# Seven-product units in four more projections of a two-layer trunk, and a second clock for the mixers' steps

## The chip, the cores and the metric

The kernel runs on one core of a Trainium2 chip. The metric is the device time of one execution in microseconds; of several runs the median counts. One run was recorded by the hardware profiler, and the profile and the trace below are of that run.

## The reference

The reference is a decoder trunk of two layers over 256 tokens of width 2048, all in float32. Cut to what matters:

```
for l in range(2):
    h = rms_norm(x)                                  # 256 x 2048
    q, k, v, uv, gate_logits = split(h @ w_in[l])    # widths 1024, 256, 256, 2048, 4096
    a = attention(rope(norm(q)), rope(norm(k)), v) @ w_attn_branch[l]
    b = spatial_gating(gelu(uv)) @ w_sgu_branch[l]
    x = x + (sigmoid(g1) * a + sigmoid(g2) * b) @ w_out[l]
    h2 = rms_norm(x)
    x = x + (silu(h2 @ w_gate[l]) * (h2 @ w_up[l])) @ w_down[l]
```

The attention has 16 query heads on 4 key heads of 64, a window of 128 and a learned sink per head. The spatial gating normalises its second half v in groups of 128 channels, mixes it over the positions of a chunk of 128 with one 128x128 matrix per group, and multiplies it by the first half u.

## The kernel before

**Matmuls.** All 256 tokens are worked on at once, as two tiles of 128. The big products are cut into jobs: one job is 1024 columns of a weight matrix (two chunks c of 512), or 512 for keys and values. A job runs over units of 512 rows of the weight; w_in has four units, the two branch projections have two. Each float32 operand is split into a high and a low part of the type that TensorE takes at full rate, and one product is three matmuls: high by high, high by low, low by high (`three`, L345). The token blocks are the stationary operand (uh, ul), the weight parts the moving one (whi, wlo).

**Weight parts.** A weight tile of 256 rows by 512 columns (128 partitions x 1024 numbers) is one part. For each part ScalarE writes the high part (whi, L226) and VectorE the low one (wlo, L234). `Stream` orders this: before the matmuls of part n, `fill` (L238) queues the low of the part four places on, and its five buffers (N_LOW) let the next low begin when the oldest part has been used.

**Whole units and seven-product units.** A whole unit of a wide job has four parts of 12 matmuls each. A job with m=1 does its first unit by Strassen's scheme instead (L371 to L390): seven parts named 11, t1, t2, 21, t3, 22, t4 of 6 matmuls each, that is 42 matmuls for 48. For it VectorE makes four differences of weight tiles (`add`, L214) and, after t4, adds a fifth product to two accumulators (L386); ScalarE copies an accumulator three times (L380) and the fifth product once (L383). The token side needs sums of its blocks, split into sh and sl, which `combine` (L450) makes once per normalised input. In the kernel before, m=1 holds for the second pair of gates, w_out and the feed-forward block, and not for queries, v, u and the first pair of gates (M_GATE at L45).

**The order of the work.** Each engine's queue follows the order in which the program names the instructions. `tick` (L296) advances a slot number by 1 after each part of a whole unit and by 0.5 after each of the seven products; `after(n, fn)` (L263) lays a step down n slots on, `soon` (L266) ahead of the next part's matmuls. The mixers' steps are laid down so: the rotation of queries and keys (`rotate`, L722), the eight groups of scores (`begin`, L775, one every Q_STEP = 4 slots, with their steps at L847), the gelu (L857), the centring of v (L888) and the spatial mixing (L919). Their results leave PSUM through three buffers (tag "at"); the big products use five accumulators.

**Jobs of a layer, in order:** keys/values (KV), queries (Q), v (V), u (U), first gates (ga0, ga1), attention branch (A0, A1), second gates and spatial branch in turn, w_out, then the feed-forward rounds. In the second layer Q comes ahead of KV. At the start of layer 0 the input is transposed on TensorE while KV runs (L595 to L601).

## Time and profile before

| | us |
|---|---|
| three runs | 2490.21, 2488.70, 2490.82 |
| median | 2490.21 |
| the profiled run, whole | 2486.52 |
| its span, first to last instruction | 2484.8 |
| TensorE busy | 2464.7 (99%) |
| VectorE busy | 1901.5 (77%) |
| ScalarE busy | 1359.2 (55%) |
| GpSimd busy | 479.5 (19%) |

A row of the timeline gives the start, the duration and the instruction, with the idle time before it and what ended it. A row of a group (by line and shape) gives the count, the busy time, the mean of one in ns and the idle time before. A row of the windows gives a stretch, its length, and each engine's busy time in it. Matmuls overlap, so what one costs is the distance between two starts and not its own duration.

### The profile page before, as it was taken

The page shows a single profiled execution, that of the slowest core. Times are in us where ns is not written, and L with a number is a line of the kernel's source. Part 1 is how long each engine was busy: PE and PEld are TensorE (multiplying, and loading weights), DVE is VectorE, ACT ScalarE, POOL GpSimd, SP SyncE. Part 2 cuts the span into 40 slices and gives each one's busy share as a digit, 9 for nine tenths or more (in the row PEclk, how much of TensorE's full clock was granted, in tenths as well). Part 3 has the DMA queues.
Part 4 walks back from the last instruction along what each step waited for, and adds up shares of the span by engine and source line. Part 5 has one row for each costly group of instructions (what it writes and reads, how often), then busy time and mean ns, then how long its engine had stood idle before and what let it go on. Part 6 is the DMA issues. An engine that isn't in the chain of part 4 may idle for free. (4 is left out here: it accounts for less than half of the span.)

```text
span 2484.8 us, 30610 instructions
## 1 busy us (share of the span) xinstructions
PE 2464.7 (99%) x11030; PEld 2023.1 (81%) x11030; DVE 1901.5 (77%) x2135; ACT 1359.2 (55%) x1660; POOL 479.5 (19%) x911
## 2 busy tenths in 40 slices
PE   9999999999999999999999999999999999999999
PEld 7888887788888888888888888877888888888887
DVE  6796667787877787777878956678878776877686
ACT  5455455576655555455654544555756555645554
POOL 1512202231220022002235122022402200220020
PEclk9999999999999999999999999999999999999999
DMA  8645656666565656566676546565756656565654
GB/s 280 227 157 169 204 196 205 205 200 223 195 233 173 234 187 233 191 219 206 216 231 214 166 160 214 192 201 187 251 189 230 211 197 209 196 221 184 213 192 164
DMA packets 161880, 507.71 MB, mean 204 GB/s; under 512 B 22016, under 2 KB 24672, under 8 KB 161728
## 3 DMA queue, kind: packets, MB, share of 16 engines
q1 hardware_dynamic: 133408, 476.87, 56.7%
q0 software_dynamic: 28000, 28.62, 3.8%
q8 instruction: 86, 1.41, 0.2%
q14 instruction: 66, 0.54, 0.1%
q10 hardware_dynamic: 320, 0.27, 0.0%
HBM read 475.27 MB, written 2.10 MB: 192 GB/s over the span
## 5 line engine op out<-in xcount | busy, mean ns | idle before, releaser
L234 DVE TENSOR_TENSOR wlo<-raw,whi 128x1024 fp32r<-128x1024 f32 (+1 forms) x940 | 1129.5, 1217 | 502.7 <-PE acc L347 415.8
L226 ACT ACTIVATE whi<-raw 128x1024 fp32r<-128x1024 f32 (+1 forms) x940 | 983.3, 1056 | 843.0 <-PE acc L348 773.6
L346 PE MATMUL acc<-whi,uh 128*128 128x512 f32 x3164 | 1243.2, 393 | 7.1 <-DVE acc L386 4.6
L347 PE MATMUL acc<-wlo,uh 128*128 128x512 f32 x3164 | 1232.7, 390 | 3.1 <-DVE wlo L234 3.1
L348 PE MATMUL acc<-whi,ul 128*128 128x512 f32 x3164 | 1232.3, 389 | 0.0
L438 POOL DMA_DIRECT2D tt<-blk x800 | 393.1, 498 | 1721.8 <-DVE blk L432 1042.6
L346 PEld LDWEIGHTS acc<-whi,uh 128*128 128x128 f32 x3164 | 594.2, 188 | 146.2 <-DVE acc L386 13.1
L348 PEld LDWEIGHTS acc<-whi,ul 128*128 128x128 f32 x3164 | 594.4, 188 | 125.0
L347 PEld LDWEIGHTS acc<-wlo,uh 128*128 128x128 f32 x3164 | 594.6, 188 | 124.0 <-DVE wlo L234 3.7
L226 ACT ACTIVATE whi<-sum 128x1024 fp32r<-128x1024 f32 x84 | 89.2, 1062 | 96.6 <-PE acc L348 61.2
L346 PE MATMUL acc<-whi,sh 128*128 128x512 f32 x336 | 132.7, 395 | 5.0 <-ACT acc L380 5.0
L347 PE MATMUL acc<-wlo,sh 128*128 128x512 f32 x336 | 131.0, 390 | 0.0
L348 PE MATMUL acc<-whi,sl 128*128 128x512 f32 x336 | 130.9, 390 | 0.0
L234 DVE TENSOR_TENSOR wlo<-sum,whi 128x1024 fp32r<-128x1024 f32 x84 | 102.5, 1221 | 8.7 <-PE acc L347 8.7
L346 PEld LDWEIGHTS acc<-whi,sh 128*128 128x128 f32 x336 | 63.0, 188 | 23.7 <-ACT acc L380 11.1
L380 ACT ACTIVATE acc<-acc 128x512 f32<-128x512 f32 x126 | 73.7, 585 | 10.0 <-PE acc L348 10.0
L348 PEld LDWEIGHTS acc<-whi,sl 128*128 128x128 f32 x336 | 63.1, 188 | 13.4
L347 PEld LDWEIGHTS acc<-wlo,sh 128*128 128x128 f32 x336 | 63.1, 188 | 12.5
L538 DVE TENSOR_TENSOR ul<-tt,uh 128x1024 fp32r<-128x1024 f32 x38 | 46.4, 1222 | 17.9 <-ACT uh L535 16.1
L535 ACT ACTIVATE uh<-tt 128x1024 fp32r<-128x1024 f32 x38 | 40.3, 1059 | 34.6 <-DMA tt<-blk 32.5
L386 DVE TENSOR_TENSOR acc<-acc,p 128x512 f32<-128x512 f32 x84 | 54.1, 689 | 0.0
L218 DVE TENSOR_TENSOR raw<-raw,sum 128x1024 f32<-128x1024 f32 x42 | 51.4, 1224 | 1.4
(134 smaller groups left out, 1055.0 us busy)
## 6 DMA issues: line engine op xcount, KB each, us to landing
raw<-in_w_in_dram SPq DMA_DIRECT2D x112, 1024.0 KB, 5.1
raw<-in_w_down_dram SPq DMA_DIRECT2D x88, 1024.0 KB, 6.7
raw<-in_w_gate_dram SPq DMA_DIRECT2D x80, 1024.0 KB, 6.0
raw<-in_w_up_dram SPq DMA_DIRECT2D x80, 1024.0 KB, 6.2
raw<-in_w_out_dram SPq DMA_DIRECT2D x32, 1024.0 KB, 6.8
tt<-blk POOLq DMA_DIRECT2D x800, 32.0 KB, 5.1
raw<-in_w_attn_branch_dram SPq DMA_DIRECT2D x16, 1024.0 KB, 6.2
raw<-in_w_sgu_branch_dram SPq DMA_DIRECT2D x16, 1024.0 KB, 5.8
```

What stands on the lines that cost most here:

```text
L218: nc.vector.tensor_tensor(out=self.raw(dst), in0=self.raw(total[0]), in1=self.raw(total[1]), op=ALU.subtract)
L226: nc.scalar.activation(hi[:, k, :], raw[:, k, :], AF.Copy)
L234: nc.vector.tensor_tensor(out=lo[:, k, :], in0=raw[:, k, :], in1=hi[:, k, :].bitcast(F32), op=ALU.subtract)
L346: nc.tensor.matmul(ps, a, hi, start=first, stop=False, skip_group_check=True)
L347: nc.tensor.matmul(ps, a, lo, start=False, stop=False, skip_group_check=True)
L348: nc.tensor.matmul(ps, b, hi, start=False, stop=last, skip_group_check=True)
L380: nc.scalar.activation({"11": x, "t2": e, "t3": y}[name], a, AF.Copy)
L386: nc.vector.tensor_tensor(out=d, in0=d, in1=fifth, op=ALU.add)
L438: nc.gpsimd.dma_start(blocks(d)[:, :, i] if whole else d[:, i].rearrange("p k t c -> p (k t) c"), src)
L535: nc.scalar.activation(blocks(unit.hi), tv, AF.Copy)
L538: nc.vector.tensor_tensor(out=blocks(unit.lo), in0=tv, in1=blocks(unit.hi).bitcast(F32), op=ALU.subtract)
```

## The change

1. Queries, v, u and the first job of the first gates get m=1 in both layers. The sums of the first token unit are therefore made early: in layer 0 at slot 4, while KV runs; in layer 1 with the unit itself, at the end of layer 0. The separate `add_sums` after the first gates goes.
2. A second clock, `calm`, counts the parts of whole units only and stands still in the seven products. The steps of rotation, scores, gelu, centring and mixing are laid down on it instead of on slots. Groups of scores follow each other every 3 steps (4 before); the transposed weights come at +8 (+6), the values at +10 (+9), the gathering of the result at +9 (+7).
3. The evictions of queries, keys, v and u go through `evicting`, which before a seven-product job spreads the second chunk over 1.5 slots.
4. The raw spatial matrices get a buffer of the big pool in place of two small ones, the small tiles of the scores get four buffers, and the eight warm-up matmuls of 128 columns become two of 512.

```diff
-Q_STEP = 4
+Q_STEP = 3
-M_GATE, M_ATT, M_SGU = (0, 0, 1, 1), (0, 0), (0, 0)
+M_Q, M_V, M_U = 1, 1, 1
+M_GATE, M_ATT, M_SGU = (1, 0, 1, 1), (0, 0), (0, 0)
...
+    def calm(n, fn):
+
+        calm_steps.append((calm_no[0] + n, fn))
...
     def tick(n=1, first=None):
         slot_no[0] += n
+        calm_no[0] += n == 1
         if first is not None:
             first()
-        due = [s for s in steps if s[0] <= slot_no[0]]
-        steps[:] = [s for s in steps if s[0] > slot_no[0]]
-        for _, fn in sorted(due, key=lambda s: s[0]):
-            fn()
+        for clock, waiting in ((slot_no, steps), (calm_no, calm_steps)):
+            due = [s for s in waiting if s[0] <= clock[0]]
+            waiting[:] = [s for s in waiting if s[0] > clock[0]]
+            for _, fn in sorted(due, key=lambda s: s[0]):
+                fn()
...
-                    after(1 + i + late, step)
-            after(9 + late, then)
+                    calm(1 + i + late, step)
+            calm(9 + late, then)
...
-                        after(n, lambda t=t, g=g: self.scores(t, g))
+                        calm(n, lambda t=t, g=g: self.scores(t, g))
                         n += Q_STEP
-                after(n + 7, lambda c=c: transposed(self.attT, c, self.att[c], sums=c == 0 and sum(M_ATT)))
+                calm(n + 9, lambda c=c: transposed(self.attT, c, self.att[c], sums=c == 0 and sum(M_ATT)))
...
-            for n, step in ((1, masked), (2, exps), (4, inverse), (6, weights), (9, values), (10, weighted)):
-                after(n, step)
+            for n, step in ((1, masked), (2, exps), (4, inverse), (8, weights), (10, values), (11, weighted)):
+                calm(n, step)
...
-            soon(halved)
+            evicting(c, halved, ahead=squared)
             for i, fn in enumerate((inner, tanh, outer)):
-                after(1 + i, fn)
+                calm(1 + i, fn)
...
-                after(4 + 3 * t + 6 * c, lambda t=t: self.center(c, t))
+                calm(4 + 3 * t + 6 * c, lambda t=t: self.center(c, t))
...
-            after(2, normed)
+            calm(2, normed)
...
+        if not l:
+            after(4, lambda nrm=norm: nrm.add_sums(0))
         for done in (kv_done, q_done)[::-1 if l else 1]:
             run(norm.units, done)
...
-        after(2, lambda nrm=norm: nrm.add_sums(0))
...
-                residual(hT, nxt, False, out if nxt is None else None)
+                residual(hT, nxt, M_Q, out if nxt is None else None)
```

More of the change, by code (lines that the diff above doesn't have):

```diff
@@ L321, in hybrid_trunk @@
     nc.scalar.activation(table, warm[:, :1], AF.Copy)
-    pw_ = ps_at.tile([P, P], F32, tag="at", name="pwarm")
-    for i in range(N_WARM):
-        nc.tensor.matmul(pw_, warm, warm, start=True, stop=True)
+    pw_ = ps_acc.tile([P, CW], F32, tag="acc4", name="pwarm")
+    for i in range(N_WARM // 4):
+        nc.tensor.matmul(pw_.rearrange("p (a b) -> p a b", b=P), warm, warm.unsqueeze(1).to_broadcast([P, 4, P]),
+                         start=True, stop=True)
     pf = ps_at.tile([P, CW], F32, tag="at", name="pf")
@@ L659, in fetch @@
             if i < 2:
-                self.wr[i] = wr_ = temp((P, 4, P), "wsraw")
+                if i == 0:
+                    self.both = slot([P, 2, 4, P], name="wsraw")
+                self.wr[i] = wr_ = self.both[:, i]
                 eng.dma_start(wr_, w_spatial[l, 4 * i:4 * i + 4].rearrange("g i j -> i g j"))
@@ L789, in scores @@
             pr4 = pr.rearrange("p i j k -> p (i j) k")
-            nm_, es, den, rd = (tiny(4, w) for w in ("negm", "es", "den", "rd"))
+            nm_, es, den, rd = (tiny(4, w, 4) for w in ("negm", "es", "den", "rd"))
             pss = []
@@ L855, in __init__, with gelu, halved, squared @@
             self.vt, self.sguT = [None] * 2, [None] * 2
-        def gelu(self, ps, dst):
+        def gelu(self, c, ps, dst):
             sq = slot([P, NT, CW], name="sq")
-            for t in range(NT):
+            def halved(t):
+                nc.vector.tensor_scalar(out=dst[:, t, :], in0=ps[t], scalar1=self.nrm.rh[t], scalar2=None, op0=ALU.mult)
+            def squared(t):
                 nc.scalar.activation(sq[:, t, :], ps[t], AF.Square, scale=self.nrm.r[t])
-            def halved():
-                for t in range(NT):
-                    nc.vector.tensor_scalar(out=dst[:, t, :], in0=ps[t], scalar1=self.nrm.rh[t], scalar2=None,
-                                            op0=ALU.mult)
             def inner():
@@ L908, in normed @@
                 nc.vector.tensor_tensor(out=vt[:, t, :], in0=vt[:, t, :], in1=self.pl.lnb[:, sl], op=ALU.add)
-            after(2, normed)
+            calm(2, normed)
         def u(self, c, ps):
             ut = slot([P, NT, CW], name="u")
-            self.gelu(ps, ut)
+            self.gelu(c, ps, ut)
             for b in range(2):
-                after(12 + 3 * b + 6 * c, lambda b=b: self.mix(c, b, ut))
-            after(19 + 6 * c, lambda: transposed(self.sguT, c, ut, sums=c == 0 and sum(M_SGU)))
+                calm(12 + 3 * b + 6 * c, lambda b=b: self.mix(c, b, ut))
+            calm(19 + 6 * c, lambda: transposed(self.sguT, c, ut, sums=c == 0 and sum(M_SGU)))
         def mix(self, c, b, ut):
@@ L933, in gated @@
                                                    op0=ALU.add, op1=ALU.mult)
-            after(1, gated)
+            calm(1, gated)
     def residual(units, nxt, sums, out_at=None, scale=None):
```

19 lines of the change are left out of this document (10 added, 9 removed).

## The prediction, made before the changed kernel ran

> **What bounds the kernel now.** I read the page first, then windows over single jobs, then the timeline of VectorE where a seven-product job begins, then the groups by shape.
>
> ```profile
> span 2484.8 us, 30610 instructions
> PE 2464.7 (99%) x11030; PEld 2023.1 (81%) x11030; DVE 1901.5 (77%) x2135; ACT 1359.2 (55%) x1660; POOL 479.5 (19%) x911
> ```
>
> TensorE is hardly ever idle. Whether the change pays hangs on two things: how many matmuls go, and whether VectorE, at 77% on average, can still feed TensorE where they go. The windows show both (length, then each engine's busy time): layer 1's queries, U, the first gates, and an existing seven-product job (gb0).
>
> ```profile
> 1248.75:1292.27 43.52, 43.52 (x193) 36.04 (x192) 28.26 (x35) 24.28 (x31) 16.72 (x35) 1.00 0.71 232
> 1359.33:1412.68 53.35, 53.35 (x274) 43.31 (x272) 50.25 (x112) 31.07 (x64) 6.62 (x4) 1.00 0.46 157
> 1412.68:1469.78 57.10, 57.10 (x298) 47.06 (x298) 41.43 (x63) 32.57 (x66) 7.91 (x16) 1.00 0.51 163
> 1561.51:1603.67 42.16, 42.16 (x187) 34.91 (x186) 26.08 (x24) 23.64 (x26) 0.00 (x0) 1.00 0.67 226
> ```
>
> A plain job of 192 matmuls takes 43.52 us, 0.2267 each; a seven-product job of 186 takes 42.16. U is 9.8 us longer than a plain job because the mixers' own matmuls stand in it, and in U VectorE is busy 50.25 of 53.35 us already. Yet lows are not late today:
>
> ```profile
> L347 PE MATMUL acc<-wlo,uh 128*128 128x512 f32 x3164 | 1232.7, 390 | 3.1 <-DVE wlo L234 3.1
> ```
>
> Those 3.1 us fall at the start of the kernel. So the gain is plain and the question is the seam, the passage into seven products. VectorE's timeline at gb0, which starts at 1561.51:
>
> ```profile
> 1561.56 1.23 DVE L234 TENSOR_TENSOR wlo<-raw,whi 128x1024 fp32r<-128x1024 f32 x1 [0.75 <-PE acc L347]
> 1562.70 1.22 DVE L218 TENSOR_TENSOR sum<-raw,raw 128x1024 f32<-128x1024 f32 x1
> 1563.84 0.68 DVE L1018 SCALAR_TENSOR_TENSOR gate<-gate,acc 128x512 f32<-128x512 f32 x1
> 1564.43 1.22 DVE L234 TENSOR_TENSOR wlo<-raw,whi 128x1024 fp32r<-128x1024 f32 x1
> 1565.57 1.22 DVE L234 TENSOR_TENSOR wlo<-sum,whi 128x1024 fp32r<-128x1024 f32 x1
> 1566.70 0.68 DVE L1018 SCALAR_TENSOR_TENSOR gate<-gate,acc 128x512 f32<-128x512 f32 x1
> 1567.30 4.62 DVE L234 TENSOR_TENSOR wlo<-raw,whi 128x1024 fp32r<-128x1024 f32 x4
> 1571.85 1.28 DVE L386 TENSOR_TENSOR acc<-acc,p 128x512 f32<-128x512 f32 x2
> ```
>
> This is the best case. VectorE had been waiting 0.75 us for a free buffer, so it is as far ahead as five buffers allow: at the job's start the lows of 11, t1, t2 and 21 lie ready and that of t3 begins. Each wide instruction holds the queue 1.14 us (1562.70 to 1563.84), a half-wide one 0.6. The seven products last 42 x 0.2267 = 9.52 us, one whole part 2.72. The fifth-product additions end at 1573.05, and TensorE needs them after t4 and one whole part, at 1561.51 + 9.52 + 2.72 = 1573.75. **The seam has 0.7 us to spare even when VectorE begins it with a full head start.** Whatever VectorE is behind at the start of seven products, less 0.7, becomes TensorE idle time. Calling the low of t3 "due" when it is needed, here it is 1561.56 + 1.2 against 1561.51 + 4 x 1.36 = 1566.95: 4.2 us ahead.
>
> **The change, part by part.**
>
> *What goes.* Eight jobs (Q, V, U, ga0 in two layers) lose 6 matmuls each: 8 x 1.36 = **10.9 us**. The Trainium skill (TensorE: Matmul & The Clock Gate, Back-to-back issue gap) gives some 131 ns as the sustained spacing of matmuls of 512 columns in a stream with weight loads; by that the 48 matmuls would be an estimated 6.3 us. The trace's 227 ns per matmul disagrees, and it decides.
>
> *What comes to VectorE.* Per job three lows more, four differences (1.14 each) and two additions (0.6 each): 9.1 us, in jobs that are 1.36 us shorter. The calm clock moves no mixer work into the seven products, but it squeezes the same work into the 12 whole parts that remain, and what stands in the last four whole parts ahead of the next seam is queued ahead of the low of t3 there. From the low of 11 to that of t3 VectorE makes four lows and two differences, 6.8 us, while the uses lie 4 x 1.36 = 5.44 apart. So
>
> lead(t3) = lead(11) + 5.44 - 6.8 - (mixer work of those four parts),
>
> with lead(11) = 9.6 at a full head start (four whole parts less one low), and the job then stalls 4.2 - lead(t3) - 0.7. The mixer work by rows of the groups:
>
> ```profile
> L893 DVE BATCH_NORM_STATS2 bst<-v 128x6 f32<-128x128 f32 x32 | 8.5, 266 | 0.0
> L894 DVE BATCH_NORM_AGGREGATE mv<-bst 128x2 f32<-128x6 f32 x32 | 5.8, 182 | 1.1
> L903 DVE TENSOR_SCALAR v<-v,mv,rv 128x128 f32<-128x128 f32 x32 | 8.8, 337 | 0.0
> L907 DVE TENSOR_TENSOR v<-v,ln 128x512 f32<-128x512 f32 x8 | 5.5, 693 | 0.3
> L803 DVE TENSOR_TENSOR pr<-psc,mask 128x512 f32<-128x512 f32 x16 | 10.3, 683 | 0.0
> L806 DVE TENSOR_REDUCE mx<-pr 128x4 f32<-128x1024 f32 x8 | 9.8, 1220 | 0.3
> L819 DVE RECIPROCAL rd<-den 128x4 f32<-128x4 f32 x16 | 2.8, 178 | 0.6
> L864 DVE TENSOR_SCALAR u<-acc,rhalf 128x512 f32<-128x512 f32 x8 | 5.6, 743 | 0.0
> L868 DVE SCALAR_TENSOR_TENSOR sq<-sq,u 128x1024 f32<-128x1024 f32 x4 | 4.9, 1216 | 0.0
> L739 DVE TENSOR_TENSOR q<-q,rq 128x1024 f32<-128x1024 f32 x4 | 4.8, 1212 | 0.0
> L745 DVE TENSOR_TENSOR sq<-q,sa 128x512 f32<-128x512 f32 x8 | 5.1, 681 | 0.0
> L750 DVE TENSOR_TENSOR q<-q,ca 128x1024 f32<-128x1024 f32 x4 | 4.9, 1216 | 0.0
> L756 DVE TENSOR_TENSOR q<-q,sq 128x1024 f32<-128x1024 f32 x4 | 5.8, 1442 | 0.0
> L432 DVE STREAM_TRANSPOSE blk<-q 128x512 f32<-128x512 f32 x8 | 5.2, 682 | 0.0
> ```
>
> Counting calm steps from KV = 8 (layer 0) gives Q 8 to 20, V to 32, U to 44, ga0 to 56, ga1 to 72; layer 1 has the same numbers from V on.
>
> - *U to ga0, both layers.* Calm 42 to 44 hold: centring of v's second chunk 4 x (266 + 182), a wide mask 2 x 683 + 1220 and small ones like the 178 ns reciprocal (0.5 together), the two evictions of u's first chunk 2 x 743, gelu's inner step 1216, normalising 4 x 337 + 2 x 693: 10.6 us, 9.5 when 0.08 is taken off for each that starts before its neighbour ends. Lead(11): in U the seam leaves the first whole part about 2 us ahead; twelve parts (32.6) and about 4.6 us of the mixers' matmuls (of U's 9.8) follow, against 12 lows, one difference and the fifth-product additions (16.0) and 15.1 us of calm 33 to 39 (four gelu steps, two centrings, two normalisings, two narrow masks of about half the wide one; overlap taken off): about 8. Lead(t3) = 8 + 5.44 - 6.8 - 9.5 = -2.9, against +4.2. Stall 6.4, of which the values matmuls that stand after the first whole part cover 0.5: **5.9**.
> - *The wait behind it.* The scores of calm 44 hold two of the three small PSUM buffers until their mask at calm 45, the values of calm 45 take the third. The weights of calm 46 must wait for that mask, which VectorE reaches after one low, centring, reciprocal, two gelu steps and half the mask: about 6 us after the additions, when TensorE is one part and the values further on (3.2). Price **2.8**, between 0 (the work already drained) and 6. Everything behind it on TensorE's queue waits too. Before, with 4 slots from scores to scores, this did not occur.
> - *V to U, layer 0.* Calm 29 to 32: rotation's 2 x 681, 1216, 1442, gathering 2 x 682, eviction of v 2 x 743 (as u), inner 1216: 8.1, less overlap 7.4. Lead(11) is 9.6 less 1.0: the two parts before carry a rotation step each and the second also a difference, 1.14 + 1.2 against 2.72 - 1.14 = 1.58 to spare. Lead(t3) = 8.6 + 5.44 - 6.8 - 7.4 = -0.2; stall **3.7**. In layer 1 the queries' rotation is long done there: no stall.
> - *KV to V, layer 1.* Calm 17 to 20 hold the second query chunk's reduction (as the 1220 one), 1216, 1442, gathering and 1212: 6.6, less overlap 6.2. Lead(11) is 9.6 less 0.7 for the same reason, with one such part. Lead(t3) = 8.9 + 5.44 - 6.8 - 6.2 = 1.3; stall **2.2**.
> - *Q to V in layer 0 and the residual to Q in layer 1:* little work ahead, **0.1** and **0.4**.
>
> *The start.* In layer 0 the sums of the first token unit are due for t1 of Q, with three differences queued by then. VectorE today, from a low that ends at 29.07 to the four-ahead low that ends at 38.97, and TensorE where t1's third matmul (the first with sl) would stand:
>
> ```profile
> 29.07:38.97 9.90, 9.90 (x48) 8.27 (x47) 8.60 (x31) 8.26 (x14) 1.76 (x2) 1.00 0.79 293
> ```
>
> ```profile
> 39.52 0.39 PE L348 MATMUL acc<-whi,ul 128*128 128x512 f32 x1
> ```
>
> ```profile
> L462 DVE TENSOR_TENSOR sums<-full 128x256 f32<-128x256 f32 x4 | 1.7, 418 | 0.0
> ```
>
> VectorE has 1.3 us of idle time in that stretch. Added are: full 1.14, four sums 4 x 0.34, sl 1.14, three differences 3.4, together 7.05; with 0.4 of the idle time filled sl is ready at 45.6. TensorE waits **6.1** (part of it earlier, since the last token unit's lows stand in the same queue). Then lows of t3 to w4 (seven, 8.0), a difference, the keys' evictions and small ones (2.9) and the additions 1.2 end at 57.7; TensorE, from 45.6, would want them at 45.6 + 0.9 + 6.8 + 2.72 = 56.0: **1.7** more. Start: 7.8.
>
> *Costed at nothing.* ScalarE's three highs and four copies per job (about 5 us; it is busy 31 to 33 of U's and ga0's 53 to 57, but where it waits for VectorE's differences, the seam's sum has that). The later gathering of the attention result (calm 68): GpSimd, busy 6.62 and 7.91 us in U's and ga0's windows, has its queue free, and by the slots the unit is there as A0's second half begins; a slot too late would cost 2.72 once per layer. The powers and gathers of rotation, on the same GpSimd queue, keep their distances in whole parts. The warm-up: same columns. More live tiles in the big pool could add waits; no row shows the price, between 0 and one VectorE step (1.2) per group of scores, and I take 0.
>
> *Sum.* Stalls 7.8 + 0.1 + 3.7 + 2 x (5.9 + 2.8) + 0.4 + 2.2 = 31.6; less 10.9: +20.7. On the profiled run, 2486.52 whole for a span of 2484.8: 2507.2. That run is 3.7 below the median of 2490.21, so the median becomes **2510.9**.
>
> **Rivals.** 0.2% of this time, 5 us, is about what a measurement can tell from no change.
> - *Seams and start covered* (faster): if under about 3.9 us of mixer work stands in the last four whole parts of each job, lead(t3) stays at 3.5 or more, and if the sums finish by 39.5 the start costs nothing. Then only 0.4 remains of the stalls: 2490.2 - 10.5 = 2479.7. For it: VectorE's average over Q to ga1 stays under TensorE's time. Against: 9.5, 7.4 and 6.2 us at three seams, by rows.
> - *Seams covered, start not:* -10.9 + 7.8 + 0.4: 2487.5, no change.
> - *The clock drops:* today TensorE has stood still 2.55 us at the start without slowing:
>
> ```profile
> 16.91 0.50 PE L347 MATMUL acc<-wlo,uh 128*128 128x512 f32 x1 [2.55 <-DVE wlo L234]
> 17.25 0.40 PE L348 MATMUL acc<-whi,ul 128*128 128x512 f32 x1
> 17.48 0.40 PE L346 MATMUL acc<-whi,uh 128*128 128x512 f32 x1
> ```
>
> The start's 6.1 us may come in one piece or two. If a longer stop slows the next 16 or so matmuls to twice 0.23, one such stop adds some 3.6 us: 2514.5. The Trainium skill (TensorE: Matmul & The Clock Gate, What's actually happening) has that rule: after an idle window of about 3.4 us the clock halves until a busy one has passed; the row above, shorter than that, does not test it.
>
> **How the numbers follow.** Forecast 0.67, covered 0.14, start alone 0.11, clock 0.08. The first and the last are slower: 0.75; no change 0.11; faster 0.14. The range: low 2490, which is the forecast without the buffer waits (5.6) and with every seam 3 us lighter (15); high 2523, the forecast with a dropped clock and a pool wait of 1.2 for each of the eight score groups. It leaves out the two covered cases.
>
> **What would show it.** TensorE idle before t1 of layer 0's Q, ended by VectorE's sl or ScalarE; rows of idle time at L346 and L347 ended by wlo and L386 in both ga0, in U of layer 0 only, in V of layer 1 only; ga1 without idle time; weights (L827) waiting after ga0's first whole parts; plain stretches of 42.17 us elsewhere. If ga0 runs without stalls, the ledger of calm 42 to 44 is wrong; if t1 does not wait, the start is.

## The result, and the profile after

| | before | after |
|---|---|---|
| median of four runs, us | 2489.45 | 2521.07 |
| lowest to highest | 2487.23 to 2490.82 | 2519.32 to 2522.96 |
| the profiled run, whole | 2486.52 | 2522.01 |
| its span | 2484.8 | 2520.3 |

The changed kernel is slower: the ratio is 1.0128, with a 95% interval of 1.0110 to 1.0146. The forecast was 2510.9 in a range of 2490 to 2523. Between the two medians the difference is 31.6 us, between the two profiled runs 35.5, where the forecast's sum had 20.7.

The page of the changed kernel, its span and the engines:

```profile
span 2520.3 us, 30675 instructions
PE 2472.7 (98%) x10970; PEld 2017.8 (80%) x10970; DVE 1971.0 (78%) x2206; ACT 1396.4 (55%) x1716; POOL 479.6 (19%) x911
```

VectorE does 69.5 us more work, but as a share of the longer span it went from 77% to 78%. An average cannot show what happened. The windows over the same four jobs as in the prediction (queries, U and first gates of layer 1, then gb0):

```profile
1271.00:1315.90 44.90, 43.27 (x187) 34.60 (x187) 35.67 (x44) 30.73 (x43) 16.78 (x35) 1.00 0.74 247
1384.80:1433.70 48.90, 47.75 (x224) 37.17 (x222) 47.83 (x88) 28.55 (x49) 8.36 (x11) 1.00 0.53 178
1433.70:1499.20 65.50, 58.49 (x297) 46.35 (x295) 54.36 (x91) 38.65 (x81) 2.29 (x4) 0.97 0.46 154
1596.90:1639.00 42.10, 42.10 (x187) 34.89 (x186) 26.10 (x24) 23.64 (x26) 0.00 (x0) 1.00 0.68 227
```

gb0 is as it was. The queries take 1.4 us more, although six matmuls went. The first gates take 8.4 us more. U takes 4.5 less, but only because mixers' matmuls moved from it into later jobs: it has 50 matmuls fewer (224 for 274), and the seven products account for 6 of them. In the first gates the granted clock is 0.97, where it was 1.00.

TensorE's groups by shape (count, busy, mean ns, then the idle time ahead of them and what ended it), first one row of the kernel before, then the changed kernel's:

```profile
L346 PE MATMUL acc<-whi,sh 128*128 128x512 f32 x336 | 132.7, 395 | 5.0 <-ACT acc L380 5.0
```

```profile
L355 PE MATMUL acc<-whi,uh 128*128 128x512 f32 x3084 | 1215.6, 394 | 8.6 <-DVE acc L395 4.9 <-ACT whi L227 1.7 <-ACT uh L498 1.6
L356 PE MATMUL acc<-wlo,uh 128*128 128x512 f32 x3084 | 1204.3, 391 | 2.8 <-DVE wlo L235 2.8
L355 PE MATMUL acc<-whi,sh 128*128 128x512 f32 x400 | 161.4, 403 | 25.3 <-ACT acc L389 24.3 <-DVE u L871 0.9
L357 PE MATMUL acc<-whi,sl 128*128 128x512 f32 x400 | 158.0, 395 | 1.3 <-DVE sl L466 1.3
L838 PE MATMUL ppt<-ident,pr 128*128 128x128 f32 x96 | 13.1, 273 | 4.1 <-DVE pr L814 4.1
```

The matmuls against the sums (whi,sh) open the products t1, t2, t3 and 22. TensorE stood idle ahead of them for 5.0 us in the kernel before, already then for ScalarE's copies (L380), and stands idle for 25.3 now. What ends the wait is not a low part (the row of wlo,uh still has 2.8) but ScalarE's copy of an accumulator, L389. Before t2 may be added to the accumulator that holds product 11, ScalarE must have copied 11 out of it; the same goes for t3. Why those copies are late is seen in ScalarE's timeline where U of layer 0 begins, at 135.20. Product 11 ends near 136.6:

```profile
136.40 0.67 ACT L874 ACTIVATE sq<-acc,rstd 128x512 f32<-128x512 f32 x1
139.00 1.06 ACT L881 ACTIVATE sq<-sq 128x1024 f32<-128x1024 f32 x1 [1.93 <-DVE sq L877]
139.97 1.04 ACT L227 ACTIVATE whi<-raw 128x1024 fp32r<-128x1024 f32 x1
140.91 0.58 ACT L389 ACTIVATE acc<-acc 128x512 f32<-128x512 f32 x1
141.43 0.66 ACT L874 ACTIVATE sq<-acc,rstd 128x512 f32<-128x512 f32 x1
143.53 1.06 ACT L227 ACTIVATE whi<-sum 128x1024 fp32r<-128x1024 f32 x1 [1.44 <-DVE sum L219]
144.50 1.04 ACT L227 ACTIVATE whi<-raw 128x1024 fp32r<-128x1024 f32 x1
145.44 0.58 ACT L389 ACTIVATE acc<-acc 128x512 f32<-128x512 f32 x1
```

The first copy (140.91) stands behind gelu's tanh (L881), which waited 1.93 us for a step of VectorE's, and behind a high part. The second (145.44) stands behind the high part of a difference that VectorE had not made. So VectorE's lateness reaches TensorE by way of ScalarE's queue, before any low part is missed. VectorE began the low of t2 at 132.97, and t2 could start only at 141.54:

```profile
132.97 1.22 DVE L235 TENSOR_TENSOR wlo<-raw,whi 128x1024 fp32r<-128x1024 f32 x1
141.54 0.80 PE L355 MATMUL acc<-whi,sh 128*128 128x512 f32 x1 [3.49 <-ACT acc L389]
```

Behind the copies stands VectorE itself. From the start of U to 204.60, near the end of ga0's seven products, it is busy for 68.23 of 69.40 us (the third of the busy times), TensorE for 61.72:

```profile
135.20:204.60 69.40, 61.72 (x263) 47.74 (x262) 68.23 (x114) 43.09 (x72) 14.15 (x19) 0.93 0.47 156
```

### The profile page after: what moved, and what is told of

Same layout as the page of the kernel before. It is cut to its first block, busy times and chain, and to the rows that moved or that the text cites. A ratio compares the mean times of both kernels' runs of the same rounds, so it can differ in the third digit from the quotient of the medians.

```text
span 2520.3 us, 30675 instructions
## 1 busy us (share of the span) xinstructions
PE 2472.7 (98%) x10970; PEld 2017.8 (80%) x10970; DVE 1971.0 (78%) x2206; ACT 1396.4 (55%) x1716; POOL 479.6 (19%) x911
## 5 line engine op out<-in xcount | busy, mean ns | idle before, releaser
L355 PE MATMUL acc<-whi,uh 128*128 128x512 f32 x3084 | 1215.6, 394 | 8.6 <-DVE acc L395 4.9
L356 PE MATMUL acc<-wlo,uh 128*128 128x512 f32 x3084 | 1204.3, 391 | 2.8 <-DVE wlo L235 2.8
L357 PE MATMUL acc<-whi,ul 128*128 128x512 f32 x3084 | 1204.2, 390 | 0.2 <-DVE ul L505 0.2
L355 PE MATMUL acc<-whi,sh 128*128 128x512 f32 x400 | 161.4, 403 | 25.3 <-ACT acc L389 24.3
L227 ACT ACTIVATE whi<-sum 128x1024 fp32r<-128x1024 f32 x100 | 106.3, 1063 | 128.0 <-PE acc L357 65.5
L357 PE MATMUL acc<-whi,sl 128*128 128x512 f32 x400 | 158.0, 395 | 1.3 <-DVE sl L466 1.3
L356 PE MATMUL acc<-wlo,sh 128*128 128x512 f32 x400 | 157.9, 395 | 0.0
L235 DVE TENSOR_TENSOR wlo<-sum,whi 128x1024 fp32r<-128x1024 f32 x100 | 122.0, 1220 | 9.3 <-PE acc L356 8.7
L355 PEld LDWEIGHTS acc<-whi,sh 128*128 128x128 f32 x400 | 76.0, 190 | 52.3 <-ACT acc L389 35.5
L389 ACT ACTIVATE acc<-acc 128x512 f32<-128x512 f32 x150 | 87.6, 584 | 11.2 <-PE acc L357 11.1
L219 DVE TENSOR_TENSOR sum<-raw,raw 128x1024 f32<-128x1024 f32 x50 | 61.4, 1228 | 0.0
L219 DVE TENSOR_TENSOR sum<-raw 128x1024 f32<-128x1024 f32 x50 | 61.0, 1220 | 0.0
```

Source lines behind the costliest of these rows:

```text
L219: nc.vector.tensor_tensor(out=self.raw(dst), in0=self.raw(total[0]), in1=self.raw(total[1]), op=ALU.subtract)
L227: nc.scalar.activation(hi[:, k, :], raw[:, k, :], AF.Copy)
L235: nc.vector.tensor_tensor(out=lo[:, k, :], in0=raw[:, k, :], in1=hi[:, k, :].bitcast(F32), op=ALU.subtract)
L355: nc.tensor.matmul(ps, a, hi, start=first, stop=False, skip_group_check=True)
L356: nc.tensor.matmul(ps, a, lo, start=False, stop=False, skip_group_check=True)
L357: nc.tensor.matmul(ps, b, hi, start=False, stop=last, skip_group_check=True)
```

## The experiments

The kernel before was measured again beside the experiments, with medians of 2486.81 to 2489.45. The ratios below are to the kernel before of the same session, and a difference of 2 or 3 us between the medians of two sessions says little. The lengths of the jobs, from the first matmul of a job to that of the next, in the profiled runs (us; layer 0, then layer 1; KV of layer 1, 21.76 in all of them, is left out):

| | KV | Q | V | U | ga0 | ga1 | Q | V | U | ga0 | ga1 |
|---|---|---|---|---|---|---|---|---|---|---|---|
| before | 29.72 | 43.67 | 45.31 | 53.35 | 57.11 | 48.21 | 43.52 | 45.29 | 53.35 | 57.11 | 48.21 |
| after | 36.20 | 46.43 | 44.53 | 53.43 | 64.79 | 54.19 | 44.90 | 47.13 | 48.82 | 65.52 | 54.19 |
| no sevens | 29.74 | 45.51 | 45.30 | 55.16 | 58.21 | 45.35 | 43.52 | 45.29 | 55.16 | 58.21 | 45.34 |
| first Q whole | 30.89 | 43.66 | 44.02 | 52.66 | 65.54 | 54.19 | 44.13 | 45.97 | 48.79 | 65.56 | 54.19 |
| ga0 whole | 32.08 | 48.21 | 44.49 | 52.66 | 69.04 | 50.95 | 44.05 | 47.45 | 48.84 | 69.26 | 50.94 |
| evictions on ScalarE | 36.51 | 46.52 | 43.94 | 51.94 | 63.98 | 54.19 | 44.07 | 45.74 | 48.58 | 64.06 | 54.19 |
| stops filled | 34.90 | 48.06 | 44.48 | 52.66 | 65.55 | 54.19 | 45.27 | 45.70 | 48.80 | 67.49 | 54.19 |
| copies first | 33.62 | 46.03 | 44.73 | 52.26 | 65.95 | 54.19 | 43.96 | 45.21 | 49.40 | 65.71 | 54.19 |
| sevens elsewhere | 29.89 | 43.65 | 43.53 | 52.13 | 60.69 | 46.04 | 43.85 | 45.70 | 51.49 | 60.70 | 46.06 |

**1. The clock and the spacing alone ("no sevens").**

```diff
-M_Q, M_V, M_U = 1, 1, 1
-M_GATE, M_ATT, M_SGU = (1, 0, 1, 1), (0, 0), (0, 0)
+M_Q, M_V, M_U = 0, 0, 0
+M_GATE, M_ATT, M_SGU = (0, 0, 1, 1), (0, 0), (0, 0)
```

> The changed kernel with queries, v, u and the first gates as plain jobs again (m=0), all else of the change kept: the second clock, the steps at 3, 8, 10, the early sums, the evictions, the new warm-up. Theory (VectorE's lead at the seams): no seam is left in V, U and ga0, so no TensorE idle time there and no halved clock there; only the early sums in KV still push the last token unit's lows, 2 to 4 us at the start. 2488 to 2494. Rival (the second clock and the 3-step spacing cost by themselves, through the three small PSUM buffers): waits of 3 to 5 us in U and ga0 of both layers remain, 2496 to 2505.

Measured: 2489.20, ratio 1.0009 (0.9999 to 1.0018). The time lies in the theory's range. U, ga0 and ga1 together take 158.7 us, as in the kernel before; the 1.8 us in layer 0's queries is a wait of TensorE for the evictions of keys and values, behind the early sums. The second clock, the spacing of three and the buffers cost next to nothing. The loss comes with the seven products.

**2. The start ("first Q whole").** Queries of layer 0 are a plain job again, and the sums of the first unit come eight slots later.

```diff
-            add_job([wl[:, o:o + CW2]], m=M_Q) if o is not None else add_job([wl[:, O_KV:O_KV + CW]])
+            add_job([wl[:, o:o + CW2]], m=M_Q if l else 0) if o is not None else add_job([wl[:, O_KV:O_KV + CW]])
...
-            after(4, lambda nrm=norm: nrm.add_sums(0))
+            after(12, lambda nrm=norm: nrm.add_sums(0))
```

> The changed kernel with layer 0's queries alone as a plain job and its sums made at slot 12 in place of 4. Theory: the waits for sl and for the last token unit's lows at the start go, KV and Q of layer 0 take together 73 to 76 us in place of 82.6 (76 if the slow clock of the first 20 us stays), all other jobs stay as they are: 2511 to 2515. Rival (the start is slow because of the new warm-up alone): KV and Q stay at 80 or more, 2518 to 2523.

Measured: 2511.74, ratio 1.0097 (1.0080 to 1.0114), which is 9.3 us below the changed kernel's median, or 7.0 when each is set against the kernel before of its own session. KV and Q together take 74.55 us for 82.63. Both lie in the theory's ranges. The start costs 8.1 us, where the forecast had 7.8 - 1.36 = 6.4. In the changed kernel TensorE stands still three times there: for the high part of the last token unit, for sl, and for the copy ahead of t3:

```profile
36.58 0.50 PE L355 MATMUL acc<-whi,uh 128*128 128x512 f32 x1 [1.62 <-ACT uh L498]
47.49 0.50 PE L357 MATMUL acc<-whi,sl 128*128 128x512 f32 x1 [1.31 <-DVE sl L466]
53.48 0.50 PE L355 MATMUL acc<-whi,sh 128*128 128x512 f32 x1 [2.06 <-ACT acc L389]
```

In ScalarE's queue, what the first and the third wait for stands behind the high part of a difference that VectorE had not made:

```profile
35.10 1.06 ACT L227 ACTIVATE whi<-sum 128x1024 fp32r<-128x1024 f32 x1 [2.78 <-DVE sum L219]
36.07 1.55 ACT L498 ACTIVATE uh<-pt,first_cols 128x256 fp32r<-128x256 f32 x4
50.94 1.06 ACT L227 ACTIVATE whi<-sum 128x1024 fp32r<-128x1024 f32 x1 [3.66 <-DVE sum L219]
52.85 0.58 ACT L389 ACTIVATE acc<-acc 128x512 f32<-128x512 f32 x1
```

The rest is the clock. In the changed kernel's KV it was halved for four windows of 3.41 us, in the kernel before for one. How many fall there differs from run to run: the kernel of experiment 3 has the same start, in its KV there was one, and KV took 32.08 us in place of 36.20 (KV and Q together 80.29 for 82.63). There sl came at 45.15, where the forecast had 45.6:

```profile
43.93 1.22 DVE L466 TENSOR_TENSOR sl<-sums,sh 128x1024 fp32r<-128x1024 f32 x1
```

**3. The first gates ("ga0 whole").**

```diff
-M_GATE, M_ATT, M_SGU = (1, 0, 1, 1), (0, 0), (0, 0)
+M_GATE, M_ATT, M_SGU = (0, 0, 1, 1), (0, 0), (0, 0)
```

> The changed kernel with the first gates' first job as a plain job in both layers. Theory: the seam's stall in ga0 (about 5.5 us a layer) and its halved clock (1.6) go, 1.36 of matmuls come back, but the wait of the weights for a small PSUM buffer stays and grows to about 5 us, since VectorE's queue of calm 42 to 45 is as long as before: 2.8 + 1.6 less per layer, 2511 to 2514. Rival (the wait for the buffer is a consequence of the seam's stall): the wait goes too, 7 to 8 us less per layer, 2504 to 2508.

Measured: 2521.23, ratio 1.0135 (1.0120 to 1.0150). Both expectations miss: taking seven products out of the costliest job wins nothing. It is 4 us longer in each layer, ga1 3.2 shorter. TensorE's groups and its timeline in layer 0's ga0 show where the wait went, and the window shows what the clock did:

```profile
L355 PE MATMUL acc<-whi,uh 128*128 128x512 f32 x3104 | 1223.1, 394 | 12.6 <-DVE acc L395 4.9 <-DVE u L871 3.7 <-ACT whi L227 1.7
L838 PE MATMUL ppt<-ident,pr 128*128 128x128 f32 x96 | 14.0, 285 | 6.9 <-DVE pr L814 6.9
```

```profile
192.69 0.50 PE L355 MATMUL acc<-whi,uh 128*128 128x512 f32 x1 [1.85 <-DVE u L871]
198.40 1.09 PE L838 MATMUL ppt<-ident,pr 128*128 128x128 f32 x4 [3.25 <-DVE pr L814]
```

```profile
193.28:203.52 10.24, 6.99 (x19) 5.17 (x18) 9.93 (x23) 3.99 (x12) 1.01 (x1) 0.50 0.09 10
```

VectorE comes out of U behind, whatever ga0 is. With seven products ga0 waits at the seam; with whole units it waits for the eviction of u (3.7 us over both layers, 0.9 in the changed kernel) and for the masks that free the small buffers (6.9, there 4.1), and the clock is halved for 10.24 us. So the loss stays with the backlog that U leaves, also where ga0 is a plain job. How much of it is the clock was not separated: the 6.99 us of matmuls in the halved stretch would take half as long at the full clock, an estimated 3.5 us less in each layer, which would bring the run close to the theory's 2514.

**4. A dose of VectorE work ahead of seams that are free.** To the kernel before, k wide subtractions into a tile that nothing reads are added ahead of fourteen seven-product jobs of the feed-forward block.

```diff
+            if n == len(job.steps) - 1:
+                dose = slot([P, CW2], name="dose") if job_no[0] in DOSE else None
+                for i in range(DOSE.get(job_no[0], 0)):
+                    nc.vector.tensor_tensor(out=dose, in0=xs[:, 0, :CW2], in1=xs[:, 1, :CW2], op=ALU.subtract)
```

> The kernel before with extra VectorE work and nothing else: k wide subtractions (1.14 us each, result unused) queued behind the last part ahead of 14 existing seams of the feed-forward block: layer 0: u0 1, u2 2, D01 3, g4 4, u4 5, u6 6, D11 7, g8 8, u8 10; layer 1: u0 2, u2 4, u4 6, u6 5, u8 3. Theory: each of these jobs, 42.17 us before, gets longer by 1.14 k - 0.7, one for one and not absorbed by later parts: 0.4, 1.6, 2.7, 3.9, 5.0, 6.1, 7.3, 8.4, 10.7; 1.6, 3.9, 6.1, 5.0, 2.7; in sum 65 us. Where the clock rule holds, the larger doses show a stretch of matmuls 0.43 apart behind the stall, 1.6 us more per halved window. Rival (VectorE catches up during the 12 whole parts that follow, so only the part of a dose above about 5 us shows): doses up to 4 cost under 1 us, in sum 20 us.

Measured: one run of 2571.27, 84.2 above the kernel before, where the theory's sum was 65 and the rival's 20. Each dosed job became longer by (us):

| k | 1 | 2 | 3 | 4 | 5 | 6 | 7 | 8 | 10 |
|---|---|---|---|---|---|---|---|---|---|
| 1.14 k - 0.7 | 0.44 | 1.58 | 2.72 | 3.86 | 5.00 | 6.14 | 7.28 | 8.42 | 10.70 |
| measured | 0.45 | 1.43, 1.43 | 2.75, 4.12 | 5.44, 5.39 | 6.59, 6.64 | 9.07, 8.01 | 10.40 | 10.44 | 12.67 |

Up to three subtractions the rule of the seam holds to 0.2 us, but for one of the five jobs. For that one and for all larger doses 1.4 to 3.1 us come on top, and there the granted clock is 0.50 behind the stop. The three stops for k = 3, 4 and again 3, and the windows behind the second and the third:

```profile
770.32 0.50 PE L347 MATMUL acc<-whi,sh 128*128 128x512 f32 x1 [2.25 <-ACT acc L381]
816.50 0.50 PE L347 MATMUL acc<-whi,sh 128*128 128x512 f32 x1 [3.51 <-ACT acc L381]
2420.75 0.50 PE L347 MATMUL acc<-whi,sh 128*128 128x512 f32 x1 [2.25 <-ACT acc L381]
```

```profile
817.52:820.94 3.42, 3.42 (x10) 2.67 (x9) 3.35 (x4) 2.78 (x4) 0.00 (x0) 0.50 0.97 353
2421.79:2425.20 3.41, 3.41 (x10) 2.64 (x9) 3.35 (x4) 2.76 (x4) 0.00 (x0) 0.50 0.91 347
```

The two stops of 2.25 us are the same to the hundredth; the first left the clock alone (2.75), the second halved it for one window (4.12). The seam is priced rightly as long as the clock stays up, and a stop above 2 us may or may not bring the clock down.

**5. VectorE's evictions on ScalarE.** The scaled evictions of queries, keys and values, v and u go to ScalarE.

```diff
-                nc.vector.tensor_scalar(out=dst[:, t, :], in0=ps[t], scalar1=self.nrm.rh[t], scalar2=None, op0=ALU.mult)
+                nc.scalar.activation(dst[:, t, :], ps[t], AF.Copy, scale=self.nrm.rh[t])
...
-            evicting(c, lambda t: nc.vector.tensor_scalar(out=dst[:, t, :], in0=ps[t], scalar1=norm.r[t], scalar2=None,
-                                                          op0=ALU.mult))
+            evicting(c, lambda t: nc.scalar.activation(dst[:, t, :], ps[t], AF.Copy, scale=norm.r[t]))
```

> The changed kernel with the evictions of queries, keys and values, v and u done by ScalarE (a scaled copy) in place of VectorE. Theory, that the seams stall because mixer work is queued on VectorE ahead of the low of t3: four evictions of about 0.7 us leave each chunk pair's last whole parts, the working of the forecast then gives 2.6 us per layer more than before in layer 0 and 1.1 in layer 1 instead of 7.9 and 6.3, so about 10 us less than the changed kernel's 2521: 2507 to 2514, with the stops of U and of the first gates shorter by 1.5 to 3 us each. Rival, that the stop is ScalarE's own (it is ScalarE's copy that TensorE is seen to wait for, and ScalarE now has more to do): 2519 to 2526.

Measured: 2515.70, ratio 1.0108 (1.0093 to 1.0123), 5.4 us below the changed kernel (4.2 when each is set against its own kernel before): between the two expectations. V, U, ga0 and layer 1's queries win 0.2 to 1.5 us each; U and ga0 of layer 0 fall together from 118.2 to 115.9. So VectorE's queue is a cause. About half of the expected 10 us is won; why the other half is not was not separated. ScalarE, for whose copies TensorE waits, now has more to do.

**6 and 7. The differences on GpSimd,** in the changed kernel and in the kernel before.

```diff
-                nc.vector.tensor_tensor(out=self.raw(dst), in0=self.raw(total[0]), in1=self.raw(total[1]),
+                nc.gpsimd.tensor_tensor(out=self.raw(dst), in0=self.raw(total[0]), in1=self.raw(total[1]),
```

> The changed kernel with the four weight differences of every seven-product job done by GpSimd in place of VectorE. Theory, that VectorE's queue is what is late and that GpSimd can make a difference in about 3 us (its mask of 512 columns takes 1.445 us): the stalls at the seams go almost wholly, 16 us less, and so do the four older waits of about 3 us at gb1 and at the first output job: 2493 to 2506. Rival, that GpSimd is the wrong place, because a difference takes over 4 us there or stands behind its gatherings, which wait for VectorE: 2525 or more, with TensorE waiting for the chain difference, high, low at each seam.

> The kernel before with its weight differences on GpSimd in place of VectorE, nothing else. Theory, that GpSimd can feed a seam in time: the four waits of about 3 us at gb1 and the first output job go, and the waits of 0.3 to 0.5 at other seams: 2489.5 falls to 2472 to 2483. Rival, that a difference on GpSimd is too slow or too late in its queue: each of the 42 or so seams waits, 2500 or more.

Measured: 2758.67 for the changed kernel (1.1086, 1.1069 to 1.1102), 2667.27 for the kernel before (1.0722, 1.0704 to 1.0740). The theory misses by far; both times fall in the rivals' ranges, though not as the second rival had it: 19 of the 42 seven-product jobs take 9 to 14 us longer than their matmuls need, the others hardly any longer. In the kernel before with this edit, rows of the timeline around one seam, GpSimd first and VectorE second:

```profile
760.26 2.39 POOL L218 TENSOR_TENSOR raw<-raw,sum 128x1024 f32<-128x1024 f32 x1 [10.76 <-DVE wlo L234]
762.61 3.38 POOL L218 TENSOR_TENSOR raw<-raw,raw 128x1024 f32<-128x1024 f32 x1
```

```profile
761.62 2.11 DVE L234 TENSOR_TENSOR wlo<-sum,whi 128x1024 fp32r<-128x1024 f32 x1 [1.50 <-PE acc L347]
764.36 2.72 DVE L234 TENSOR_TENSOR wlo<-raw,whi 128x1024 fp32r<-128x1024 f32 x1 [0.62 <-PE acc L347]
```

A difference takes 2.4 us there, twice VectorE's time, and it also holds VectorE up. The low that starts at 761.62 ends at 763.73, 1.1 after GpSimd's first difference; the one at 764.36 ends at 767.08, 1.1 after the second; and the second took a microsecond longer, the time of that first low. One waits for the whole of the other. The Trainium skill (SBUF — State Buffer, Who interferes with whom) says that a VectorE instruction with two inputs in SBUF contends with a GpSimd instruction that reads SBUF, and that the ports they share are locked by one of the two at a time; the trace agrees, with these four rows.

**8 and 9. Stops filled with matmuls by zeros,** so that TensorE does not stand still and the clock stays up.

```diff
+                for _ in range(FILL.get((job_no[0] - 1, name), 0)):
+                    nc.tensor.matmul(q[:P // 2], zeros, unit.hi[:, 0:2, :], start=False, stop=False, skip_group_check=True)
```

> The changed kernel with matmuls by a block of zeros put into the stops (10 and 4 ahead of t2 and t3 in U of layer 0, 8 and 4 in both first gate jobs, 6 ahead of t3 in V of layer 1), so that no stop there is longer than about 2.5 us and the clock is not halved; they add nothing to the sums. Theory, that a halved clock costs little where VectorE is later still (after the halved stretch of the first gates TensorE waits for t3 once more): only V of layer 1 and a part of U are won, 1.5 to 4.5 us: 2516.5 to 2519.5. Rival, that each halved window adds its 1.6 us to the total (five windows): 2511 to 2514.

Measured: 2534.61, ratio 1.0186 (1.0171 to 1.0201), 13.5 above the changed kernel and outside both expectations. The filler ahead of t3 wrote to the accumulator of t1, which ScalarE copies after 21, so it had to wait for one more copy: U, V of layer 1 and the two ga0 grew by 2.6 to 3.3 us each (12.1 together). It says nothing of the clock, but it shows that one more step of waiting on ScalarE's queue costs about 3 us at a seam. In the second version the filler ahead of t3 writes to the accumulator of 21:

```diff
-                    nc.tensor.matmul(q[:P // 2], zeros, unit.hi[:, 0:2, :], start=False, stop=False, skip_group_check=True)
+                    nc.tensor.matmul((x if name == "t3" else q)[:P // 2], zeros, unit.hi[:, 0:2, :], start=False, stop=False, skip_group_check=True)
```

> The changed kernel once more with matmuls by a block of zeros in the stops, now written to accumulators on which nothing waits (ahead of t2 into that of t1, ahead of t3 into that of 21): 10 and 4 in U of layer 0, 8 and 6 in both first gate jobs, 6 in V of layer 1. The earlier filler ahead of t3 had to wait for ScalarE's copy of the fifth product and so measured that. Theory, that after a halved stretch VectorE is still behind, so that the clock's price is mostly hidden: 2516.5 to 2520.5, with the stop ahead of t3 growing by what the clock no longer takes. Rival, that each of the five halved windows adds its 1.6 us: 2511 to 2514.

Measured: 2521.42, ratio 1.0134 (1.0120 to 1.0147), 0.35 above the changed kernel (3.0 when each is set against its own kernel before): the theory, a little worse than its range. The same window of layer 0's ga0, first in the changed kernel, then with the filler:

```profile
195.27:198.69 3.42, 3.42 (x10) 2.65 (x9) 3.42 (x4) 0.68 (x2) 0.00 (x0) 0.50 0.00 0
```

```profile
195.27:198.69 3.42, 3.42 (x16) 2.56 (x16) 3.42 (x4) 0.69 (x2) 0.00 (x0) 1.00 0.00 0
```

The clock stays at 1.00, and in U, in V and in layer 0's ga0 no window is halved any more. The stop ahead of t3, first in the changed kernel and then with the filler, is no earlier:

```profile
200.71 0.51 PE L355 MATMUL acc<-whi,sh 128*128 128x512 f32 x1 [1.22 <-ACT acc L389]
```

```profile
197.86 1.54 PE L387 MATMUL acc<-uh,zeros 128*64 128x512 f32 x6
200.81 0.51 PE L358 MATMUL acc<-whi,sh 128*128 128x512 f32 x1 [1.40 <-ACT acc L394]
```

From the start of ga0 (188.60 and 187.93) t3 comes after 12.1 and 12.9 us: the 0.8 us that U of layer 0 wins is lost again in ga0. U and ga0 of layer 0 take 118.2 us together in the changed kernel with three halved windows, 118.2 in experiment 2 with two, and 118.2 here with none. Where VectorE is late in any case, a halved clock only fills time in which TensorE would wait. V of layer 1 is the exception: it took 47.13 us with a halved window, and without one 45.70 here and 45.97 in experiment 2. ga0 of layer 1 takes 2.0 longer, where its wait for the buffers now halves the clock.

**10. Seven products where VectorE is free ("sevens elsewhere").** Queries of layer 0, U and ga0 plain, ga1 with seven products, evictions on ScalarE as in 5, sums as in 2.

```diff
-M_Q, M_V, M_U = 1, 1, 1
-M_GATE, M_ATT, M_SGU = (1, 0, 1, 1), (0, 0), (0, 0)
+M_Q, M_V, M_U = 1, 1, 0
+M_GATE, M_ATT, M_SGU = (0, 1, 1, 1), (0, 0), (0, 0)
```

> A version from the experiments: seven products only where VectorE has little queued ahead of the seam: V in both layers, queries of layer 1, and the second attention gates (plain in both kernels so far); queries of layer 0, U and the first gates stay plain; evictions of queries, keys and values, v and u on ScalarE; the mixers' spacing of three on the calm clock as in the changed kernel. Theory: five jobs lose 6 matmuls, 6.8 us, stalls of about 1 us in layer 1 and some 2 us for the other clock and spacing as the run without any of the new seven-product jobs had: 2483 to 2487 where the kernel before takes 2488.5. Rival, that seams stall here too, by 2 us and more each: 2490 to 2500.

Measured: 2487.09 beside 2486.81 for the kernel before, ratio 0.9998 (0.9989 to 1.0007). That is in neither range: the theory's gain of 1.5 to 5.5 us does not come, nor the rival's loss. V of layer 0 wins 1.8, but queries and V of layer 1 are 0.3 and 0.4 longer although each lost 1.36 us of matmuls, and U, ga0 and ga1 together are 0.2 longer in layer 0 and 0.4 shorter in layer 1. In layer 1 the seams take back all that the matmuls give.

**11 and 12. The copies ahead of the high parts ("copies first").** The high part of t3 is queued behind the copy of 11, that of t4 behind the copy after t2; in the changed kernel, then in the version of 10.

```diff
-                if len(self.highs) < min(upto + 1, n) and self.summed > len(self.highs):
+                if (len(self.highs) < min(upto + 1, n) and self.summed > len(self.highs)
+                        and held.get(len(self.highs), -1) < self.at):
...
+        if job.m:
+            for late, copy in (("t3", "11"), ("t4", "t2")):
+                held[first + names.index(late)] = first + names.index(copy)
```

> The changed kernel with one order changed on ScalarE: the high part of t3 is queued behind the copy of product 11 and that of t4 behind the copy after t2, in every seven-product job (before, each copy stood behind a high part that waits for VectorE's difference). Nothing is left out. Theory, that part of each stop is the order on ScalarE and not VectorE's lateness: the waits ahead of t3 in queries, V, U and the first gates fall by 1 to 2 us each, and so do the four older ones of 1.3 us ahead of t3 at gb1 and the first output job; 8 to 14 us less than the changed kernel: 2507 to 2513. Rival, that VectorE is late in any case and the wait only reappears at the low part of t3 or t4 or at the additions of the fifth product: 2518 to 2523.

> The version with seven products in V, in layer 1's queries and in the second gates, evictions on ScalarE, and now the same order on ScalarE (high parts of t3 and t4 behind the copies). Theory of the order: the older waits at gb1 and the first output job lose 1.3 us each (four of them), those of layer 1's queries and V about 1 each: 2479 to 2483 where the kernel before takes 2488.5 and the version without the new order took 2487. Rival, VectorE's lateness: 2485 to 2489, no change.

Measured: 2573.56 (1.0335, 1.0321 to 1.0349) and 2544.62 (1.0224, 1.0210 to 1.0238). Both expectations miss; the groups of the first say why:

```profile
L364 PE MATMUL acc<-whi,uh 128*128 128x512 f32 x3084 | 1215.0, 394 | 76.2 <-ACT acc L398 68.1 <-DVE acc L404 4.8 <-ACT whi L227 1.7
L364 PE MATMUL acc<-whi,sh 128*128 128x512 f32 x400 | 157.2, 393 | 10.3 <-ACT acc L398 7.9 <-DVE u L880 2.4
```

The wait ahead of the sums' products falls from 25.3 to 10.3, 15.0 us, as the theory had it (the old waits ahead of t3 at gb1 and the first output job are gone). But the wait ahead of the plain products rises from 8.6 to 76.2. The net is 67.6 - 15.0 = 52.6 us more idle time; the profiled run is 48.4 us longer, the median 52.5. The new wait stands ahead of t4, in nearly every seven-product job: gb0, which lost nothing before, now loses 1.7 us. ScalarE's timeline at gb1 of layer 0:

```profile
418.06 0.58 ACT L398 ACTIVATE acc<-acc 128x512 f32<-128x512 f32 x1 [0.23 <-PE acc L366]
418.55 1.05 ACT L227 ACTIVATE whi<-sum 128x1024 fp32r<-128x1024 f32 x1
419.50 2.00 ACT L227 ACTIVATE whi<-raw 128x1024 fp32r<-128x1024 f32 x2
421.40 0.59 ACT L401 ACTIVATE p<-acc 128x512 f32<-128x512 f32 x1
421.87 1.06 ACT L227 ACTIVATE whi<-raw 128x1024 fp32r<-128x1024 f32 x1
422.82 0.60 ACT L398 ACTIVATE acc<-acc 128x512 f32<-128x512 f32 x1
```

The copy after t2 (418.06) comes at once, but the high parts held back until then run as a block and the copy after t3 (422.82) waits behind them. Holding t3's high part alone was not tried. In the new seven-product jobs the order brings little: from their first matmul to the first of their whole parts V and queries of layer 1 now lose 2.2 and 1.7 us in place of 4.1 and 2.4, but U and ga0 of layer 0 still take 52.26 + 65.95 = 118.2 us.

## Why the prediction was right, and where its sizes were off

The sign held, and the main of the mechanism: VectorE's head start at the seam runs out, and the waits of TensorE exceed the 10.9 us that 48 matmuls give. The groups bear out the count: 3164 - 3084 = 80 fewer plain matmuls and 400 - 336 = 64 more with sums in each of three kinds, that is 48. The next table has what each seam lost in the changed kernel: the distance from the job's first matmul to the first of its whole parts, less the 9.52 us of 42 matmuls. For the start it is the length of KV and Q over that of the kernel before, and 1.36; for the buffers it is the stop. The last column has the same for experiment 9, where past KV no window of these stretches is halved.

| place | forecast | measured | stops filled |
|---|---|---|---|
| start: KV and Q of layer 0 | 7.8 | 10.6 (82.63 - 73.39 + 1.36) | 10.9 |
| V, layer 0 | 0.1 | 1.4 | 1.4 |
| U, layer 0 | 3.7 | 6.6 | 5.8 |
| seam of ga0, layers 0 and 1 | 5.9, 5.9 | 7.0, 7.7 | 7.7, 8.1 |
| buffers behind it | 2.8, 2.8 | 2.1, 2.1 | 2.1, 2.1 |
| Q, layer 1 | 0.4 | 2.4 | 2.8 |
| V, layer 1 | 2.2 | 4.1 | 2.7 |
| U, layer 1 | 0 | 1.9 | 1.9 |

The measured column adds up to 45.9, of the 46.4 that make the 35.5 us (35.5 + 10.9); the forecast had 31.6.

- *The gain and the seam rule were right.* The dose shows the rule with its 0.7 us to spare to within 0.2 us for one, two and three subtractions, as long as the clock stays up.
- *The named seams had the right cause and were sized too light*, with the clock up U of layer 0 by 2.1, ga0 by 1.8 and 2.2, V of layer 1 by 0.5. (The terms listed for calm 42 to 44 add up to 10.3 and not 10.6, which would make ga0 5.6.) In U and ga0 the cause is VectorE's work: VectorE is busy for 98% of the stretch shown above, and the 118.2 us of U and ga0 in layer 0 stay whether the clock is halved or not and whichever of two orders ScalarE has, and fall to 115.9 when VectorE is relieved of the evictions. With ga0 whole the loss stays, so it is the backlog from U that ga0 pays for.
- *"Costed at nothing" is the step that failed.* The prediction held that where ScalarE "waits for VectorE's differences, the seam's sum has that". The sum asked when the low of t3 is due. TensorE asks earlier, for the copies ahead of t2 and t3, and in ScalarE's queue there stand ahead of them high parts of differences and gelu's tanh, each waiting for VectorE. So the seams that were costed near nothing (V of layer 0, Q and U of layer 1) cost 1.4, 2.4 and 1.9. The kernel before had this path already, in the 5.0 us ahead of whi,sh that end with L380. Experiment 11 shows that the order on ScalarE is a cause of its own for layer 1's queries and V, and not for U and ga0 of layer 0.
- *The start* came near the forecast in experiment 3, where the clock was halved less: sl came at 45.15 for 45.6, and KV and Q lost 80.29 - 73.39 + 1.36 = 8.3 for 7.8. But in the changed kernel TensorE's waits stood at the last token unit and ahead of t3 as well, by way of ScalarE, and not at the additions.
- *What would show it:* idle rows were named at the lows and the fifth additions (wlo and L386). They are at the copies. ga1 has no idle time and the weights (now L838) wait behind ga0's first whole parts, as said.
- *The rival of the clock* had 0.08. The clock did drop, in nine windows where the kernel before has one. Also the stop of 2.55 us at the start, which the prediction saw pass without slowing, was followed by a halved window in the changed kernel. But with the other stops filled the time stayed at 2521.4, so the clock does not explain the missing 15 us: in U and ga0 of layer 0 it costs nothing, in V of layer 1 1.4, at the start 2.3 (82.63 for 80.29). The dose shows that its price is real (1.4 to 3.1 us a job) where nothing else is late.
- *Seams and start covered* (2479.7) is refuted by the result, and experiment 1 shows that the seven products are what costs: the same clocks and spacing without them take 2489.2.
- *Luck.* That 2521.07 falls inside the range owes something to luck. The range's upper end was made of a dropped clock (3.6) and of pool waits (9.6; with the forecast's 2510.9 that is 2524.1, not 2523). No wait for the pool shows in U and ga0, where VectorE is hardly ever idle; the distance was filled by the seams, each up to 2.9 us above its forecast, and by the start.

What stays open: how a version with only t3's high part held would do, how much of ga0's loss in experiment 3 is the halved clock, and why experiment 5 won only half of what was expected.

## What to carry to other kernels

Before a step that needs an engine far ahead, follow every queue through which its result passes: here TensorE waited for ScalarE's copies, which stood behind other work that waited for VectorE. A saving of 1.36 us a job is lost to two wide VectorE instructions too many (1.43 us in the dose), so such a form is worth its place only where the feeding engine is idle ahead of it. And a backlog moves: taking the expensive form out of the job that waits does not help while the job ahead of it leaves the engine behind.

## What the runs showed of the hardware

- The clock falls on a fixed grid. In the dosed kernel the halved windows that start at 817.52 and 2421.79 are 1604.27 us apart, 470 times 3.4133. The Trainium skill (TensorE: Matmul & The Clock Gate, What's actually happening) has a free-running window of about 3.4 us and says that the clock halves after an idle one. The grid agrees; the idle time does not have to fill a window, since a stop of 2.25 us halved the clock in one job and not in another.
- GpSimd and VectorE, each with two inputs in SBUF, ran one after the other: GpSimd's 2.39 us became 3.38 and VectorE's 1.22 up to 2.72.
